# A hybrid attention and MLP layer on one core: how many steps of a side computation each attention unit carries

## The chip, the core and the metric

One core of a Trainium2 chip runs the whole layer in one launch. The core has a matrix engine (TensorE, PE in the profile, with its weight loads shown apart as PEld), a vector engine (VectorE, DVE), a scalar engine (ScalarE, ACT), a general engine (GpSimd, POOL) and an engine that here only issues transfers (SyncE, SP). Each engine works through its own queue in order. The metric is the device time of one execution in microseconds (us).

## What is computed

One trunk layer for a batch of one sequence: 2048 tokens of width 1024, all in float32. Cut to what matters here:

```
mod = silu(c) @ w_ada + b_ada                       # 1 x 6144, six parts of 1024
shift_a, scale_a, gate_a, shift_m, scale_m, gate_m = split(mod, 6)
h = rms_norm(x, g_attn) * (1 + scale_a) + shift_a
q_f, k_f, v_f, q_s, k_s, v_s, f_logit = split(h @ w_in)
o_fox = forgetting_attention(...)                   # 8 heads of 64, causal
o_sb  = stick_breaking_attention(...)               # 8 heads of 64, causal
x = x + gate_a * (concat(head_norm(o_fox), head_norm(o_sb)) @ w_out)
h = rms_norm(x, g_mlp) * (1 + scale_m) + shift_m
u_gate, u_val = split(causal_depthwise_conv(h @ w_up))
x = x + gate_m * ((silu(u_gate) * u_val) @ w_down)
return rms_norm(x, g_final)
```

The conditioning vector c is one row, so each of the six parts of mod is a product of a 1 x 1024 row with a 1024 x 1024 matrix. The first two parts (shift_a, scale_a) are needed at once and are computed at the start. The other four are the *late modulation*: gate_a (part 2 in the code), gate_m (part 5), shift_m (part 3) and scale_m (part 4). Gate_a is multiplied into the rows of w_out (with the head norms' gains), which then serves the output projection. The other three are needed only for the MLP.

## The kernel before

**Attention in 32 units.** A unit is one kind of attention ("sb" for stick-breaking, "fox" for forgetting), one pair of heads p (0 to 3) and one block tb of 512 queries (0 to 3). The list `units` (L807) has them in the order sb before fox, then p, then tb, so units 0 to 15 are sb and 16 to 31 are fox, and every fourth unit has the same tb. Attention is causal, so the work of a unit grows with tb: `tri` (L846) puts it at 10 + 16 tb, and `weight` (L843) puts an sb unit 1.4 times higher. `attend` (L697) is a generator that yields after each small stretch of a unit: logits, an elementwise stage on ACT, DVE and POOL, transposes on PE, copies out of PSUM, and products with the values.

**Projections beside it.** Each unit needs its queries and keys (and every second p also the values) projected from the normalized tokens. `proj` (L463) does it unit by unit: eight tiles `hp` of 512 KB are loaded from scratch memory `hs` (L468) and multiplied on PE (L342, L413). This runs ahead of attention: `pace` (L849) states how many projection steps should have been emitted at each point of a unit, and `follow` (L1058) emits them. For PE these products are the filler that runs while attention waits for ACT and DVE. The last projection ends in unit 26.

**The late modulation.** `late_mod` (L756) is a third generator. Its first step (the convolution's weights) is taken in unit 4 (L1035). After it come 55 steps:

- part 2: steps 1 to 8 each load one 128 x 1024 row block of w_ada (L776, 512 KB), scale it on ACT (L782, two halves) and add it into `wsum` on POOL (L783, two halves; the first block is L780 on POOL alone). Steps 9 and 10 sum over the partitions with two products on PE (L790) and add the bias (`gt`, loaded at L787) on DVE (L791)
- steps 11 to 26: `fold_out` (L743). Every second step loads a block of w_out (L746); every step scales half of it on DVE (L749), splits it into a high and a low float on ACT and POOL (L45, L46) and stores it to `wos` (L753)
- part 5: steps 27 to 34 are the loads and sums, 35 and 36 the products of the gate; then gt is stored to `gate_m` (L796)
- part 3: steps 37 to 44 are the sums, 45 the column sums on PE (L800, 16 small matmuls in the trace) with an addition on DVE
- part 4: steps 46 to 53 and 54 in the same way; step 55 is a last small operation on DVE

**One pool of ten tiles.** The projection's eight tiles and everything wide in the late modulation come from the same ten buffers named `hp`: `h_tile` (L155) and `wide` (L158), which is h_tile under another shape. A buffer is free again when the last instruction that reads it is done. So `wsum` holds one buffer from the first sum until the product on PE, and `gt` one from its load until it has been used up.

**Order of the instructions.** `interleave` (L109) decides in what order instructions are emitted. After each yield of attention it lets the projections follow and then takes steps from each filler: with k steps for a unit of n yields, step j (from 0) is taken after the first yield i for which (i + 1) k / n is above j. The framework then schedules each engine's queue with a simulation of its own, where the order of emission is the priority: an instruction that is ready and has its buffers can be put ahead of earlier ones that are not, on its own engine. The queues made this way are fixed when the program runs.

**After unit 29.** Ahead of unit 30 the rest of late_mod is drained (L1050), the pool of the hp tiles is closed, and the pool `big` takes its space; `first_mix` (L939) loads the folded w_out into it (`wo`, L948) during unit 30, and the output projection (L912) begins in unit 31.

```
for i, u in enumerate(units):
    ...
    interleave(attend(...), n, [(lm if i >= LATE else None, PER, False), (tail, ..., True)], follow)
```

with `LATE, PER = 12, 3` (L862): three steps in each of the units 12 to 29, which makes 54 by the end of unit 29, and the last one in the drain.

Of the kernel before, what the change touches and what calls it, by code (L numbers as in the profile page):

```python
# [34 lines left out]
def kernel(ctx: ExitStack, tc: tile.TileContext, x, c, w_ada, b_ada, g_attn, w_in, b_fgate,  # L35
# [69 lines left out]
    def drain(g):  # L105
        for _ in g:
            pass

    def interleave(main, n, fillers, follow):  # L109
        live = [[g, k, 0] for g, k, _ in fillers if g is not None]  # L110
        for i, _ in enumerate(main):
            tick()
            follow(i)
            for e in live:
                while e[2] < (i + 1) * e[1] / n:
                    e[2] += 1
                    if next(e[0], StopIteration) is StopIteration:
                        e[2] = 1 << 30
        for g, _, whole in fillers:
            if g is not None and whole:  # L120
                drain(g)
# [3 lines left out]
    def open_pool(name, side=None, space=None):  # L125
        st = pools[name] = ExitStack()
        kw = dict(space=space) if space is not None else {}
        return st.enter_context(tc.tile_pool(name=name, bufs=1, side=side, reuse_waits="tile", **kw))

    def close_pool(*names):  # L130
        for name in names:
            pools.pop(name).close()
# [84 lines left out]
    b = pv()  # L217
# [6 lines left out]
    for r, src in ((R_GA, g_attn), (R_GM, g_mlp), (R_GF, g_out_fox), (R_GS, g_out_sb), (R_BA, b_ada)):  # L224
        n = src.shape[1] // P
# [465 lines left out]
    def tick(n=1):  # L691
        for d in deferred:
            d[1] -= n
        while deferred and deferred[0][1] <= 0:
            deferred.pop(0)[0]()
# [111 lines left out]
    units = [(k, p, tb) for k in ("sb", "fox") for p in range(4) for tb in range(NTB)]  # L807
    weights = {}
    results = {}
# [16 lines left out]
    def attend_steps(u):  # L826
        kind, p, tb = u
        if kind == "fox":
            return sum(2 * (2 + 2 * tb + j2 + 1) for j2 in range(2)) + 1
        return sum(2 * (tb + 1 + 2 * tb + j2 + 1) for j2 in range(2)) + 1  # L830
# [3 lines left out]
    def project():  # L834
        for u in units[1:]:
            for _ in proj_gen(u):
                projected[0] += 1
                yield
            projected[1] += 1

    ahead = project()

    def weight(u):  # L843
        return 1.4 * tri(u[2]) if u[0] == "sb" else tri(u[2])

    def tri(tb):  # L846
        return 10 + 16 * tb
# [11 lines left out]
                      base + (total - base) * (done + weight(units[i]) * m / n) / span if i >= START else 0)  # L859

    LAG, ENDQ = 12, 16
    LATE, PER = 12, 3  # L862
    START, STOP = 3, 30

    HT = 2 * P
# [150 lines left out]
    IDLE = 6  # L1016
# [9 lines left out]
    lm = late_mod()  # L1026
    Fbs = None
    tail = None
    big = orp = None
    for i, u in enumerate(units):  # L1030
        kind, p, tb = u
        nxt = units[i + 1] if i + 1 < len(units) else None
        if u == ("sb", 1, 0):
            forget_sums()
            next(lm)  # L1035
        if u == ("fox", 0, 0):
            close_pool("sx")
            sx = open_pool("fx", side="right")
        if i == 14 or (kind == "fox" and tb == 0 and p):
            Fbs = load_sums(p if kind == "fox" else 0)  # L1040
        n = attend_steps(u)
        if i >= len(units) - 2:
            head_root(i - len(units) + 2)
            head_scale(i - len(units) + 2, pt(), sx)
        if nxt is None:
            tail = first_out()
        if i == len(units) - 2:
            for _ in ahead:
                projected[0] += 1
            drain(lm)  # L1050
            close_pool("sl", "psa")
            psc = open_pool("psc", side="right", space=PSUM)
            big = open_pool("big")
            orp = open_pool("orp")
            tail = first_mix()
        goals = list(pace(i))

        def follow(m):  # L1058
            while projected[0] < goals[min(m, n - 1)]:
                with tc.issue_after(marks[max(0, len(marks) - 1 - LAG)]) if START <= i < ENDQ else nullcontext():  # L1060
                    if next(ahead, 1) is not None:
                        break
            if nxt and projected[1] > i + 1 and loaded_units[0] == i + 1:
                loaded_units[0] += 1
                load_unit(*nxt, results[nxt[:2]])

        interleave(attend(kind, p, tb, results[kind, p], Fbs), n, [(lm if i >= LATE else None, PER, False), (tail, 17 + IDLE if nxt is None else 13, True)], follow)
        while nxt and loaded_units[0] == i + 1:
            next(ahead, None)
            follow(n)  # L1070
# [225 lines left out]
    for u in range(1, NU):  # L1296
        for c in range(8 if u == 1 else 0, 16):
            t, n, q = chunk(u, c)
# [8 lines left out]
    def bank_a():  # L1307
        return bank(psd, "o", 4)
# [138 lines left out]
    for sblk, order in enumerate(orders):  # L1447
# [21 lines left out]
        for n, ci in enumerate(order):  # L1469
# [5 lines left out]
            if not last_pair:  # L1475
                nxt = weights(n + 1)
            elif sblk == 0:
                load_h(1, 0)
                back = w_reload(SAVE[0])
                nxt = islice(back, 5)  # L1480
            else:
                nxt = None
# [12 lines left out]
        a, b = bank_a(), bank_a()  # L1495
# [189 lines left out]
    for i in range(7):  # L1685
        nxt = {}
        kept = []
        for s in range(2):
            banks = set_banks(s)
            xhs_ = [None] * 4  # L1690
            tail = []
            left = i in lefts
            if left:
                half, n = lefts[i]
                ops = left_over(s, half)
            for kp in range(NKP):
                a = ahead_a.pop((i, s, kp), None)
                if a is None:
                    a = a_operand(i, s, kp, raw_a())
# [63 lines left out]
```

## Time and profile before

| what | us |
|---|---|
| time, median of 3 runs | 2950.44 |
| lowest and highest of the runs | 2949.66, 2955.75 |
| span of the profiled execution, first to last instruction | 2941.4 |
| the median run's time less the profiled span | 9.0 |
| PE busy in the span | 2867.8 |
| ends of units 11, 14, 15, 17, 18, 19 (store of the unit's output, L740) | 686.0, 801.5, 882.8, 922.7, 978.5, 1058.9 |
| ends of units 23 to 26 | 1217.1, 1241.8, 1283.6, 1337.3 |
| ends of units 27 to 31 | 1379.4, 1391.0, 1419.1, 1453.7, 1516.9 |
| first and last load of w_ada by late_mod (L776) | 629.7, 1308.4 |

The profile is of one execution, and its engines' rows say how much of the span each was at work. PE is busy almost throughout; what matters are the few places where it isn't. The span is what the views below divide up; the time of a run has some 9 us more around it. After attention (from 1516.9 us) come the output projection and the MLP, where the change does nothing.

### The profile page before, as it was taken

The page shows a single profiled execution, that of the slowest core. Times are in us where ns is not written, and L with a number is a line of the kernel's source. Part 1 is how long each engine was busy: PE and PEld are TensorE (multiplying, and loading weights), DVE is VectorE, ACT ScalarE, POOL GpSimd, SP SyncE. Part 2 cuts the span into 40 slices and gives each one's busy share as a digit, 9 for nine tenths or more (in the row PEclk, how much of TensorE's full clock was granted, in tenths as well). Part 3 has the DMA queues.
Part 4 walks back from the last instruction along what each step waited for, and adds up shares of the span by engine and source line. Part 5 has one row for each costly group of instructions (what it writes and reads, how often), then busy time and mean ns, then how long its engine had stood idle before and what let it go on. Part 6 is the DMA issues. An engine that isn't in the chain of part 4 may idle for free.

```text
span 2941.4 us, 45922 instructions
## 1 busy us (share of the span) xinstructions
PE 2867.8 (97%) x15772; PEld 2459.7 (84%) x15772; DVE 2179.5 (74%) x3464; ACT 1686.0 (57%) x3187; POOL 901.1 (31%) x967
## 2 busy tenths in 40 slices
PE   8999999999999999999999999999999999999998
PEld 7888888888988988888888788888788888888887
DVE  5787778877886656658843788888998888575476
ACT  5776767677776656658744554444444445433342
POOL 0431322243032423231213344444254543142200
PEclk8999999999999999999999999999999999999999
DMA  9749756867469794794537775554754444975644
GB/s 293 255 139 321 236 188 207 301 211 229 162 212 356 269 277 139 232 323 140 182 120 233 245 232 128 130 136 129 236 132 125 130 130 132 309 257 185 216 158 151
DMA packets 348346, 601.89 MB, mean 205 GB/s; under 512 B 34672, under 2 KB 178800, under 8 KB 348112
## 3 DMA queue, kind: packets, MB, share of 16 engines
q1 hardware_dynamic: 324208, 558.06, 57.7%
q0 software_dynamic: 10880, 20.97, 4.3%
q10 hardware_dynamic: 13024, 19.93, 1.9%
q8 instruction: 124, 2.03, 0.3%
q14 instruction: 110, 0.90, 0.1%
HBM read 420.77 MB, written 177.02 MB: 203 GB/s over the span
## 4 chain that ended last, share of the span: by engine, by line
PE 46%; DMA 3%; DVE 2%; SPq 1%; ACT 1%; issue 1%; POOL 0%; DVEq 0%; ACTq 0%; POOLq 0%
PE ps_o L1315 19%; PE ps_t L1315 7%; PE ps_o L1614 6%; PE ps_t L1614 3%; PE ps_bc L1614 3%; PE ps_o L912 1%; PE ps_pv L615 1%; DMA r<-rstd 1%; PE ps_bc L912 1%; PE ps_pt L606 1%; PE ps_o L1609 1%; DMA wo<-wos 1%; DMA hm<-hf_m 1%; SPq L895 1%; DVE op L46 1%
## 5 line engine op out<-in xcount | busy, mean ns | idle before, releaser
L1315 PE MATMUL ps_o<-op,wu 128*128 128x512 f32 x2592 | 608.0, 389 | 2.0 <-DVE snap L1366 1.5
L1315 PEld LDWEIGHTS ps_o<-op,wu 128*128 128x128 f32 x2592 | 486.2, 188 | 103.9 <-DVE snap L1366 1.9
L611 DVE TENSOR_TENSOR at<-ps_pt,at 128x512 fp32r<-128x512 f32 (+1 forms) x576 | 366.1, 652 | 100.2 <-ACT at L610 97.3
L636 DVE TENSOR_TENSOR_SCAN a<-r,a 128x512 f32<-128x512 f32 (+2 forms) x320 | 368.3, 1167 | 77.8 <-ACT a L631 39.9
L342 PE MATMUL ps_pj<-hp,w_qk 128*128 128x512 f32 x1512 | 411.2, 403 | 14.5 <-DMA hp<-hs 12.9
L610 ACT ACTIVATE at<-ps_pt 128x512 fp32r<-128x512 f32 (+1 forms) x576 | 318.5, 576 | 139.1 <-PE ps_pt L606 123.1
L615 PE MATMUL ps_pv<-at,V 128*128 128x256 f32 x2216 | 386.8, 292 | 9.3 <-DVE at L611 4.2
L615 PEld LDWEIGHTS ps_pv<-at,V 128*128 128x128 f32 x2216 | 320.9, 190 | 39.8 <-DVE at L611 11.4
L342 PEld LDWEIGHTS ps_pj<-hp,w_qk 128*128 128x128 f32 x1512 | 275.4, 190 | 71.0 <-DMA hp<-hs 16.2
L45 ACT ACTIVATE wu<-wuraw 128x512 fp32r<-128x512 f32 x204 | 128.9, 632 | 248.5 <-PE ps_o L1315 190.1
L596 PE MATMUL ps_qk<-K,Q 128*128 128x512 f32 (+2 forms) x640 | 265.7, 416 | 5.6 <-ACT a L631 3.3
L413 PE MATMUL ps_pj<-w_v,hp 128*128 128x256 f32 (+1 forms) x1536 | 236.6, 288 | 2.1 <-DVE hp L422 1.6
L597 PE MATMUL ps_qk<-K,Q 128*128 128x512 f32 (+2 forms) x640 | 235.7, 369 | 0.0
L1315 PE MATMUL ps_t<-op,wu 128*128 128x512 f32 x888 | 220.8, 390 | 1.0 <-DVE op L46 1.0
L413 PEld LDWEIGHTS ps_pj<-w_v,hp 128*128 128x128 f32 x1536 | 209.0, 189 | 10.9 <-DVE q L373 1.5
L630 ACT ACTIVATE r<-ps_qk 128x512 f32<-128x512 f32 (+2 forms) x320 | 173.1, 541 | 58.2 <-PE ps_qk L597 55.5
L46 DVE TENSOR_TENSOR wu<-wuraw,wu 128x512 fp32r<-128x512 f32 x204 | 189.6, 930 | 18.1 <-ACT wu L45 16.7
L1315 PEld LDWEIGHTS ps_t<-op,wu 128*128 128x128 f32 x888 | 166.4, 188 | 36.5 <-DVE op L46 1.8
L606 PE MATMUL ps_pt<-edge,a 128*128 128x128 f32 x1088 | 185.1, 274 | 8.4 <-DVE a L636 7.8
L1614 PE MATMUL ps_o<-op 128*128 128x512 f32 x840 | 191.5, 389 | 0.0
L1614 PEld LDWEIGHTS ps_o<-op 128*128 128x128 f32 x840 | 157.7, 188 | 32.7
L679 ACT ACTIVATE p<-p,mn 128x128 f32<-128x128 f32 (+15 forms) x128 | 153.9, 1203 | 53.3 <-DVE mn L675 52.2
(342 smaller groups left out, 5237.6 us busy)
## 6 DMA issues: line engine op xcount, KB each, us to landing
hp<-hs SPq DMA_DIRECT2D x224, 512.0 KB
wuraw<-in_w_up_dram SPq DMA_DIRECT2D x80, 512.0 KB
ra<-g SPq DMA_DIRECT2D x136, 256.0 KB
rb<-in_w_down_dram SPq DMA_DIRECT2D x108, 256.0 KB
g<-u SPq DMA_DIRECT2D x80, 256.0 KB
hs<-hp SPq DMA_DIRECT2D x32, 512.0 KB
hp<-in_w_ada_dram SPq DMA_DIRECT2D x32, 512.0 KB
qk_fox<-q SPq DMA_DIRECT2D x32, 512.0 KB
```

The lines of the kernel that those rows point to most:

```text
L46: (lo_engine or nc.gpsimd).tensor_sub(lo, src, f(hi))
L342: nc.tensor.matmul(acc, w[kt][:, a, n], h[:, bb], start=kt == 0 and i == 0, stop=kt == KT - 1 and i == 2)
L413: nc.tensor.matmul(av[:, t * width:(t + 1) * width], hts[kt][:, a, tok], w[1][kt][:, bb, 0:width], start=kt == 0 and m == 0, stop=kt == KT ...
L596: nc.tensor.matmul(b[:, :cw], Q[:, hl, 0, qcols], K[:, hl, :cw], start=True, stop=False)
L597: marks.append(nc.tensor.matmul(b[:, :cw], Q[:, hl, 1, qcols], K[:, hl, :cw], start=False, stop=True).ins)
L606: nc.tensor.transpose(b[:, i * P:(i + 1) * P], blk(kts[kk], qi), ident)
L610: copies = [nc.scalar.activation(at[:, 0, lo:], b[:, lo:], AF.Copy).ins, nc.vector.tensor_sub(at[:, 1, lo:], b[:, lo:], f(at[:, 0, lo:])).ins]
L611: nc.vector.tensor_sub(at[:, 1, lo:], b[:, lo:], f(at[:, 0, lo:])).ins]
L615: m = nc.tensor.matmul(o[:, 0:2 * P], V[kt // 4][:, kt % 4, hl, :], rhs, start=first and kk == 0 and w == 0, stop=last and kk == 1 and w == 1)
L636: nc.vector.tensor_tensor_scan(rev, r[:, 0:need][:, ::-1], rev, 0.0 if right[qi] is None else right[qi][:, 0:1], ALU.mult, ALU.add)
L1315: nc.tensor.matmul(b, w[:, p, j], o[:, q], start=first and i == 0, stop=last and i == 2, skip_group_check=True)
L1614: nc.tensor.matmul(b, a[:, p, t * P:(t + 1) * P], w[:, q], start=first and i == 0, stop=last and i == 2, skip_group_check=True)
```

## The change

The constant three is replaced by a number of steps for each unit, `late_steps(i)`, and the steps are spread over units 12 to 28 in proportion to `weight`:

```diff
+    def late_steps(i):
+        upto = [sum(weight(u) for u in units[LATE:max(LATE, min(v, LATE_END))]) for v in (i, i + 1, LATE_END)]
+        a, b = (round(LATE_STEPS * v / upto[2]) for v in upto[:2])
+        return b - a
+
...
-    LATE, PER = 12, 3
+    LATE, LATE_END, LATE_STEPS = 12, 29, 55
...
-        interleave(attend(kind, p, tb, results[kind, p], Fbs), n, [(lm if i >= LATE else None, PER, False), (tail, 17 + IDLE if nxt is None else 13, True)], follow)
+        interleave(attend(kind, p, tb, results[kind, p], Fbs), n, [(lm, late_steps(i), False), (tail, 17 + IDLE if nxt is None else 13, True)], follow)
```

The weights of units 12 to 28 sum to 608.4, and the cumulated, rounded share of 55 gives these numbers (in the column "emitted", the steps taken by the end of the unit, before and after):

| unit | kind, p, tb | steps before | steps after | emitted before | emitted after |
|---|---|---|---|---|---|
| 12 | sb 3 0 | 3 | 1 | 3 | 1 |
| 13 | sb 3 1 | 3 | 4 | 6 | 5 |
| 14 | sb 3 2 | 3 | 5 | 9 | 10 |
| 15 | sb 3 3 | 3 | 7 | 12 | 17 |
| 16 | fox 0 0 | 3 | 1 | 15 | 18 |
| 17 | fox 0 1 | 3 | 2 | 18 | 20 |
| 18 | fox 0 2 | 3 | 4 | 21 | 24 |
| 19 | fox 0 3 | 3 | 6 | 24 | 30 |
| 20 | fox 1 0 | 3 | 0 | 27 | 30 |
| 21 | fox 1 1 | 3 | 3 | 30 | 33 |
| 22 | fox 1 2 | 3 | 4 | 33 | 37 |
| 23 | fox 1 3 | 3 | 5 | 36 | 42 |
| 24 | fox 2 0 | 3 | 1 | 39 | 43 |
| 25 | fox 2 1 | 3 | 2 | 42 | 45 |
| 26 | fox 2 2 | 3 | 4 | 45 | 49 |
| 27 | fox 2 3 | 3 | 5 | 48 | 54 |
| 28 | fox 3 0 | 3 | 1 | 51 | 55 |
| 29 | fox 3 1 | 3 | 0 | 54 | 55 |

No instruction is added or removed; the steps are emitted at other places.

## The prediction

> **What bounds the kernel now.** I read the page first, then who made PE wait in the stretch where the late modulation runs, then those waits in order of time, then a table of stretches, and last SP's queue.
>
> ```profile
> span 2941.4 us, 45922 instructions
> ...
> PE 2867.8 (97%) x15772; PEld 2459.7 (84%) x15772; DVE 2179.5 (74%) x3464; ACT 1686.0 (57%) x3187; POOL 901.1 (31%) x967
> ...
> PEclk8999999999999999999999999999999999999999
> ```
>
> PE is at work 97% of the span at nearly full clock, and the change adds and removes no instruction. So it can only win or lose time in which PE stands still or runs slowly. The waits of PE from 600 to 1420 us (units 11 to 29; columns: total us, times, longest):
>
> ```profile
> PE ps_pj L342 <- DMA hp<-hs: 12.3, 7, 6.0
> ```
>
> It is the largest row: a projection waits for its tiles, the tiles that share ten buffers with the late modulation. The three long ones of the fox units, from PE's timeline:
>
> ```profile
> 1052.80 0.80 PE L342 MATMUL ps_pj<-hp,w_qk 128*128 128x512 f32 x1 [6.01 <-DMA hp<-hs]
> ...
> 1155.19 1.66 PE L342 MATMUL ps_pj<-hp,w_qk 128*128 128x512 f32 x6 [0.47 <-DMA hp<-hs]
> 1208.81 0.79 PE L342 MATMUL ps_pj<-hp,w_qk 128*128 128x512 f32 x1 [3.40 <-DMA hp<-hs]
> ```
>
> A stall costs more than its length, as the table of stretches shows (length, then busy us of PE, PEld, DVE, ACT, POOL, then granted clock, DMA share, GB/s):
>
> ```profile
> 1040.00:1052.80 12.80, 6.79 (x54) 6.26 (x52) 5.45 (x16) 6.55 (x17) 2.20 (x4) 0.93 1.03 307
> 1052.80:1058.90 6.10, 6.10 (x20) 5.15 (x21) 1.04 (x4) 1.31 (x3) 0.30 (x1) 0.58 1.05 275
> ...
> 1208.80:1217.00 8.20, 8.19 (x37) 7.49 (x38) 3.61 (x9) 5.73 (x16) 3.52 (x4) 0.63 0.65 250
> ...
> 1167.70:1195.00 27.30, 27.09 (x192) 24.22 (x191) 26.14 (x66) 20.93 (x35) 3.77 (x7) 1.00 0.25 81
> ```
>
> After the stall in unit 19 the clock is 0.58 for 6.1 us: 6.1 x 0.42 = 2.6 us lost on top of 6.0. After the one in unit 23 it is 0.63 for 8.2 us: 8.2 x 0.37 = 3.0 us on top of 3.4. The two have different causes: DMA is full (a share of 1.03) ahead of the first, and nearly idle (0.25) ahead of the second.
>
> **Why unit 23 stalls.** SP's loads of one projection's tiles (L468) between 1120 and 1201 us, grouped, with the times of the first and the last; then pieces of SP's queue: the ends of units 21 and 22 (L740), the bias's load (L787), the seventh tile, the gate's store (L796) and the eighth tile:
>
> ```profile
> L468 SPq DMA_DIRECT2D hp<-hs x8: 319/339/450, 1126.7 to 1200.7; - x8
> ```
>
> ```profile
> 1087.76 0.73 SPq L787 DMA_DIRECT2D hp<-in_b_ada_dram  x1
> ...
> 1115.10 0.32 SPq L740 DMA_DIRECT2D os<-oT  x1
> ...
> 1151.16 0.34 SPq L468 DMA_DIRECT2D hp<-hs  x1
> ...
> 1167.74 0.34 SPq L740 DMA_DIRECT2D os<-oT  x1
> ...
> 1198.70 0.33 SPq L796 DMA_DIRECT2D gate_m<-hp  x1
> ...
> 1200.74 0.33 SPq L468 DMA_DIRECT2D hp<-hs  x1
> ```
>
> POOL's first sums of parts 5 and 3, and the products on PE that end part 5's gate and part 4's column sums:
>
> ```profile
> 1003.89 1.57 POOL L780 TENSOR_SCALAR hp<-hp,cs 128x512 f32<-128x512 f32 x1 [2.81 <-DMA hp<-in_w_ada_dram]
> ...
> 1129.54 3.12 POOL L780 TENSOR_SCALAR hp<-hp,cs 128x512 f32<-128x512 f32 x2 [2.66 <-PE ps_qk L597]
> ```
>
> ```profile
> 1179.91 1.02 PE L790 MATMUL ps_pt<-hp,ones 128*128 128x512 f32 x2
> ...
> 1195.49 1.02 PE L790 MATMUL ps_pt<-hp,ones 128*128 128x512 f32 x2
> ...
> 1403.53 1.84 PE L800 MATMUL ps_pt<-ones,hp 128*128 128x1 f32 x16
> ```
>
> Count the buffers at 1151: seven tiles of the projection are loaded; part 5's wsum has one since 1003.9, its gt since 1087.8, part 3's wsum since 1129.5. That is ten. The eighth tile, wanted after the six products of 1155.2, is loaded at 1200.7, once the gate's products (1179.9, 1195.5) have let wsum go. In between the projection stands still; L342's instructions on PE alone, in the table of stretches (length, PE busy, clock, DMA share, GB/s):
>
> ```profile
> 1155.70:1208.80 53.10, 1.15 (x5) 0.99 0.46 130
> ```
>
> That is 1.15 us of projection in 53. So the sums run early, as soon as buffers allow, while the products that free the buffers run where they are emitted. I check that: steps 35 and 36 are taken in unit 23 (1167.7 to 1217.1) after 33% and 67%, which is 1184 and 1200; they ran at 1180 and 1195. Step 54 in unit 29 (1391.0 to 1419.1) after 67% is 1410; it ran at 1404. The place of emission tells when PE's steps run, within some 6 us.
>
> **The change, part by part.**
>
> *Part 5's gate.* Its loads and POOL's additions, grouped (duration ns min/median/max, first and last start):
>
> ```profile
> L776 SPq DMA_DIRECT2D hp<-in_w_ada_dram x8: 328/333/628, 997.9 to 1077.2; - x8
> ...
> L783 POOL TENSOR_TENSOR hp<-hp x14: 1290/1298/1308, 1011.5 to 1082.8; 128x512 f32<-128x512 f32 x14
> ```
>
> Steps 35 and 36 move to unit 22 (1115.1 to 1167.7), after 25% and 50% of it: 1128 and 1141. The two buffers come free some 55 us earlier, before the eighth tile is due. The stall goes: 3.4 idle + 3.0 of slow clock + 0.5 at 1155.2 = 6.9 us. Is PE then late for something else? PE takes its queue in a fixed order, so products that met an unfinished sum would hold attention's matmuls behind them and with them ACT and DVE; the sums must be ready by 1128. They were done by 1082.8 + 1.3 = 1084, and are emitted earlier now. What is late next is attention's own chain; what filler in the empty 53 us would save further I leave at 0, since PE shows busy 27.09 of 27.30 us in 1167.7 to 1195 without any. **-6.9**, from 0 (another tile is late there) to -6.9.
>
> *Part 5's sums and unit 19.* Ahead of 1052.8 the load of the last three tiles stands in SP's queue behind transfers that take long on full DMA engines:
>
> ```profile
> 1041.12 4.49 SPq L363 DMA_DIRECT2D K<-qk_fox  x4
> 1045.92 2.54 SPq L468 DMA_DIRECT2D hp<-hs  x3
> ```
>
> ```profile
> L753 SPq DMA_DIRECT2D wos<-hp x16: 525/560/871, 802.9 to 997.3; - x16
> ```
>
> Part 5's eight loads of 512 KB (4.2 MB, 14 us at the 307 GB/s above) run beside them from 998 to 1077, right behind fold_out's last store at 997.3. After the change fold_out's last step is in unit 19 after 17% instead of unit 20 after 33%, and steps 27 to 30 are in unit 19. So the burst can begin some 10 to 20 us sooner, if fold_out ends sooner. It then collides less at 1040, but it stays in unit 19, and SP's order is new. I take half of the stall's 6.0 + 2.6: **-4**, from -8.6 to +8.6 (a second one like it).
>
> *Fold_out in unit 15.* Seven steps are emitted there instead of three. DVE and ACT are loaded there (units 15, then 16 with 17; below, fold_out's operations on DVE in unit 15):
>
> ```profile
> 801.50:882.80 81.30, 76.37 (x515) 67.93 (x514) 67.45 (x109) 63.88 (x140) 24.89 (x34) 1.00 0.67 222
> 882.80:922.70 39.90, 39.82 (x254) 35.09 (x253) 30.27 (x79) 26.93 (x54) 11.48 (x16) 1.00 1.04 370
> ```
>
> ```profile
> L749 DVE SCALAR_TENSOR_TENSOR hp<-hp,cols 128x512 f32<-128x512 f32 x4 | 2.8, 748 | 1.7 <-DMA hp<-in_w_out_dram 1.7
> ```
>
> Four steps of fold_out already ran in unit 15, pulled forward, so three more come: 3 x 0.75 = 2.2 us on DVE, 3 x 0.43 waiting for w_out (1.7 over 4). Projections cover part of it. **+1.5**, from 0 to +3.5. The steps that leave units 16 and 17 win nothing: PE is busy 39.82 of 39.90 us there.
>
> *Part 4's column sum.* It moves from unit 29 (1403.5) to unit 27 (1337.3 to 1379.4) after 80%, 1371. The chain of waits goes through it:
>
> ```profile
> 1403.69 1.68 PE ps_pt L800 x16
> ...
> 1406.40 6.35 DMA wo<-wos
> ```
>
> ```profile
> 1379.40:1419.10 39.70, 37.35 (x260) 31.74 (x259) 33.77 (x99) 32.65 (x65) 8.60 (x18) 1.00 0.69 220
> 1419.10:1453.70 34.60, 31.96 (x216) 26.98 (x214) 31.34 (x84) 28.74 (x54) 10.15 (x16) 1.00 0.60 196
> ```
>
> The loads of wo can begin 30 us earlier and clear SP before first_mix. But wo is used in unit 31, after 1453.7, and PE's idle time from unit 28 to 30 is 2.35 + 2.64 us in all, with DVE busy 85 to 91%. **-1**, from 0 to -5.0. Part 3's column sum moves from unit 26 to unit 25 and frees a buffer; no tile is late there now: 0. Part 2's gate products stay in units 14 and 15 or move into the end of 14: 0, from -2.4 (what is left of the 12.3 us) to +2.4.
>
> Sum: -6.9 - 4 + 1.5 - 1 = -10.4 us on the profiled span of 2941.4, which becomes 2931; with the 9.0 us around it, 2940 against the median of 2950.4.
>
> *A rule against the rows.* The Trainium skill (TensorE: Matmul & The Clock Gate, Part 1) says that PE falls to half clock after an idle window of about 3.4 us and is back at full clock after about 3.4 us of work. By that a stall would cost half of 3.4, 1.7 us as an estimate, beyond its length, the first term 5.6 instead of 6.9, the second 3.9, and the sum -9.0. The rows show 2.6 and 3.0, so I keep those.
>
> **The rivals.**
>
> *The stall only moves* (to 2949): the change does not do what it says, since the sums float anyway. Ten buffers for eight tiles and up to three wide ones stay ten; with steps emitted in units 19 and 23 in greater number, another eighth tile can be late in place of this one. For it: the 12.3 us are seven waits, not one. Against: the holders are let go earlier everywhere. Then only -1 is left.
>
> *Slower by DMA* (to 2959). DMA is full in units 16 and 17 (1.04 in the row above) and nearly so in 18:
>
> ```profile
> 922.70:978.50 55.80, 55.80 (x335) 49.16 (x334) 35.48 (x84) 30.32 (x57) 12.83 (x17) 1.00 0.93 337
> ```
>
> If fold_out ends early enough for part 5's 4.2 MB to go out ahead of the tiles that SP loads up to 975, that is 12 us of transfers at 337 GB/s ahead of a projection without spare buffers: a stall like that of 1052.8, 8.6 us, with nothing won elsewhere. It decides from a first load of part 5 before about 970; before the change it was 998. With unit 23's gain beside it, 2952.
>
> *Slower by POOL and DVE* (2952 to 2959). POOL's sums take longer beside stick-breaking (620 to 750 us, first row) than beside fox (1120 to 1330):
>
> ```profile
> L783 POOL TENSOR_TENSOR hp<-hp 128x512 f32<-128x512 f32 x14 | 21.3, 1541 | 20.7 <-ACT hp L782 20.7
> ...
> L783 POOL TENSOR_TENSOR hp<-hp 128x512 f32<-128x512 f32 x28 | 35.7, 1294 | 22.6 <-ACT hp L782 19.7 <-issue 2.8
> ```
>
> ```profile
> L783 POOL TENSOR_TENSOR hp<-hp x56: 1267/1293/2204, 644.6 to 1322.3; 128x512 f32<-128x512 f32 x56
> ```
>
> If it is DVE that holds POOL up and the reverse, three more steps in unit 15 could hold DVE by up to 3 x (0.75 + 2.2) = 8.8 us (2.2 for the longest sum, 2204 ns). DVE has 81.3 - 67.5 = 13.8 us to spare, so it decides only if the holds fall into the scan's chain. The Trainium skill (SBUF — State Buffer, Who interferes with whom) says that a DVE instruction with two SBUF inputs contends with a GpSimd instruction that reads SBUF; by that rule, the two means above agree in direction, and no run here shows the lock itself.
>
> **How the numbers follow.** Forecast 0.48; the stall moves 0.27; DMA 0.17; POOL and DVE 0.08. A measurement of this kernel can tell about 0.2%, 5.9 us, from no change: 2944.5 to 2956.3. The forecast's own range, 2931 to 2947, is mostly below it (0.42 of 0.48); the second rival lies mostly inside (0.24 of 0.27); of the last two 0.16 of 0.25 is above. That makes 0.46 faster, 0.36 the same, 0.18 slower. The range from 2930 to 2960 takes in all bounds but both stalls gone with every other term at its best, and two new stalls.
>
> **What would show it.** Right: L790's second pair near 1130 to 1145, all eight tiles of that projection loaded by 1150, no wait of L342 above 2 us in unit 23, clock 1.00 there, L800's last group near 1370. Wrong: L342's waits again above 10 us in total, elsewhere; or a clock under 0.9 in units 16 to 19; or unit 15 longer than 84 us.

## The result and the profile after

| what | before | after |
|---|---|---|
| median of 8 runs, us | 2949.55 | 2958.06 |
| lowest and highest | 2939.44, 2955.75 | 2955.62, 2965.59 |
| ratio, 95% interval | | 1.0032 [1.0021, 1.0042] |
| a second set of runs, ratio (median 2954.91) | | 1.0024 [1.0015, 1.0034] |

The change makes the kernel slower by 7 to 9 us; the forecast was 10.4 us faster. All runs count here and below but one, a slow one of g2 (3810.77 us at a granted clock of 0.69). The page of the changed kernel, whose profiled run took 2959.57 us:

```profile
span 2957.1 us, 45920 instructions
...
PE 2871.1 (97%) x15772; PEld 2467.8 (83%) x15772; DVE 2182.6 (74%) x3464; ACT 1682.5 (57%) x3187; POOL 911.0 (31%) x967
...
PEclk9999999999999999999999999999999999999999
```

The work is the same, as the counts show. PE is busy 3.3 us longer than before and stands idle 12.4 us longer (span less busy: 73.6 before, 86.0 after).

**Where the time came from.** A unit's store moves against its work, so the stretches here are cut at the same point of the program in every kernel: where DVE has written the last output of units 10, 15, 19, 26 and 30. First the kernel before, then the changed one, in the table of stretches (length, then busy us of PE, PEld, DVE, ACT, POOL, then granted clock, DMA share, GB/s):

```profile
607.60:873.50 265.90, 253.16 (x1695) 225.42 (x1693) 207.53 (x280) 198.57 (x432) 79.78 (x97) 1.00 0.61 197
873.50:1058.40 184.90, 178.26 (x1124) 158.44 (x1124) 119.09 (x299) 113.86 (x226) 59.64 (x79) 0.98 0.91 308
1058.40:1336.90 278.50, 273.64 (x1818) 246.88 (x1817) 179.30 (x462) 177.54 (x339) 86.32 (x112) 0.99 0.70 231
1336.90:1453.20 116.30, 110.78 (x772) 96.04 (x771) 102.22 (x278) 95.49 (x183) 26.29 (x49) 1.00 0.61 192
sum 845.60, PE 815.85 PEld 726.78 DVE 608.15 ACT 585.45 POOL 252.04; mean PE 203.96 PEld 181.69 DVE 152.04 ACT 146.36 POOL 63.01
```

```profile
612.30:883.70 271.40, 256.30 (x1690) 229.22 (x1688) 214.67 (x288) 200.25 (x439) 89.12 (x101) 0.97 0.62 202
883.70:1065.80 182.10, 175.45 (x1111) 156.74 (x1111) 113.38 (x286) 113.08 (x221) 61.37 (x79) 0.98 0.89 302
1065.80:1347.10 281.30, 276.47 (x1832) 249.24 (x1831) 179.92 (x468) 175.12 (x337) 79.62 (x108) 0.99 0.69 226
1347.10:1470.30 123.20, 112.39 (x776) 99.79 (x774) 102.14 (x278) 96.11 (x183) 26.16 (x49) 0.96 0.59 181
sum 858.00, PE 820.61 PEld 735.00 DVE 610.11 ACT 584.56 POOL 256.28; mean PE 205.15 PEld 183.75 DVE 152.53 ACT 146.14 POOL 64.07
```

From unit 11 to unit 30 the changed kernel takes 12.4 us longer: +5.5 in units 11 to 15, -2.8 in 16 to 19, +2.8 in 20 to 26, +6.9 in 27 to 30. PE's busy time alone grows by 4.8 for (nearly) the same instructions: the clock in units 11 to 15 is 0.97 in place of 1.00, so 256.3 us of work hold what 253.2 held. In the second execution of the changed kernel the four stretches are 271.2, 181.3, 280.6 and 117.6, so the last +6.9 are not in every execution. The other 3.3 us between the two spans lie where the change moves no step: +4.7 ahead of unit 11, -1.4 behind unit 30.

**How much two traces can differ by chance.** Up to 664 us every engine's queue is the same in all twenty traces of this case, and the stretch ahead of unit 11 takes 607.6 to 621.8 us. Five of them (the kernel before, e2, e4, e6, e8 below) have the same queues on through unit 15, but for one small instruction on POOL, and take 263.1 to 269.1 us for units 11 to 15. A difference of some 6 us in one stretch of two traces can be scatter. Five traces with the changed kernel's queues in units 11 to 15 take 268.8 to 271.4 us.

**The gate's products went where the forecast put them, and the stall came back elsewhere.** The changed kernel's products of part 5, and its loads of tiles from 1120 us (duration ns min/median/max, first and last start):

```profile
L790 PE MATMUL ps_pt<-hp,ones x4: 590/592/592, 1126.2 to 1136.3; 128*128 128x512 f32 x4
```

```profile
L468 SPq DMA_DIRECT2D hp<-hs x17: 319/376/1196, 1137.0 to 1237.1; - x17
```

The products are 50 us earlier and the eighth tile is loaded at 1137 in place of 1200.7: the count of buffers was right. But PE's waits from 600 to 1440 us (total, times, longest) read

```profile
PE ps_pj L342 <- DMA hp<-hs: 13.2, 5, 5.6
PE ps_pv L615 <- DVE oT L738: 8.2, 2, 7.4
PE ps_pt L606 <- DVE a L636: 6.9, 10, 1.9
```

against 12.3 of L342 before. Unit 19 still holds one of 5.6, and the one of unit 23 is now in PE's timeline 18 us later, and costs the clock what it did before (0.60 for 8.5 us, with DMA now full):

```profile
1226.75 1.04 PE L342 MATMUL ps_pj<-hp,w_qk 128*128 128x512 f32 x3 [3.02 <-DMA hp<-hs]
1229.09 1.65 PE L342 MATMUL ps_pj<-hp,w_qk 128*128 128x512 f32 x3 [1.30 <-DMA hp<-hs]
```

```profile
1220.00:1227.50 7.50, 4.47 (x36) 3.98 (x34) 2.73 (x11) 5.31 (x11) 2.50 (x5) 1.00 1.01 308
1227.50:1236.00 8.50, 7.20 (x31) 6.15 (x31) 2.91 (x5) 2.28 (x6) 1.11 (x1) 0.60 1.04 293
```

The other two rows are new or larger: 7.4 us of waiting for oT in unit 29, and twice as much waiting for the scan (a, L636), which in the kernel before reads

```profile
PE ps_pt L606 <- DVE a L636: 3.6, 7, 1.1
```

The experiments take up both.

### The profile page after: what moved, and what is told of

The parts are those of the page before. It is cut to its first block, busy times and chain, and to the rows that moved or that the text cites. A ratio compares the mean times of both kernels' runs of the same rounds, so it can differ in the third digit from the quotient of the medians.

```text
span 2957.1 us, 45920 instructions
## 1 busy us (share of the span) xinstructions
PE 2871.1 (97%) x15772; PEld 2467.8 (83%) x15772; DVE 2182.6 (74%) x3464; ACT 1682.5 (57%) x3187; POOL 911.0 (31%) x967
## 4 chain that ended last, share of the span: by engine, by line
PE 48%; DMA 2%; DVE 2%; ACT 1%; issue 1%; SPq 0%; POOL 0%; DVEq 0%; ACTq 0%; POOLq 0%
PE ps_o L1320 20%; PE ps_t L1320 8%; PE ps_o L1619 6%; PE ps_t L1619 3%; PE ps_bc L1619 3%; PE ps_o L917 2%; PE ps_pv L615 1%; PE ps_pt L606 1%; PE ps_bc L917 1%; DMA r<-rstd 1%; PE ps_o L1614 1%; PE ps_qk L596 1%; PE ps_qk L597 1%; DMA os<-oT 0%; DMA x1s<-x1u 0%
## 5 line engine op out<-in xcount | busy, mean ns | idle before, releaser
L342 PE MATMUL ps_pj<-hp,w_qk 128*128 128x512 f32 x1512 | 417.1, 405 | 17.6 <-DMA hp<-hs 13.8
L636 DVE TENSOR_TENSOR_SCAN a<-r,a 128x512 f32<-128x512 f32 (+2 forms) x320 | 370.3, 1173 | 82.1 <-ACT a L631 42.0
L342 PEld LDWEIGHTS ps_pj<-hp,w_qk 128*128 128x128 f32 x1512 | 274.9, 191 | 72.7 <-DMA hp<-hs 16.3
```

The costliest lines, as they stand in the source:

```text
L342: nc.tensor.matmul(acc, w[kt][:, a, n], h[:, bb], start=kt == 0 and i == 0, stop=kt == KT - 1 and i == 2)
L636: nc.vector.tensor_tensor_scan(rev, r[:, 0:need][:, ::-1], rev, 0.0 if right[qi] is None else right[qi][:, 0:1], ALU.mult, ALU.add)
```

## The experiments

Three theories at first. A: wo's loads, set free earlier, stand ahead of unit 27's store in SP's queue, and attention waits for the buffer of oT. B: the moved sums cost projection waits in units 12 to 26. C: the loss is spread, a part of it in units 12 to 15. Where an edit changes only numbers of steps, they are given in words as a map from unit to steps; a unit that is not named keeps its own.

**The last units (theory A).** SP's queue of the changed kernel, then the wait that follows on DVE and on PE, and the clock:

```profile
1389.16 1.89 SPq L953 DMA_DIRECT2D wo<-wos  x3
...
1392.03 1.76 SPq L953 DMA_DIRECT2D wo<-wos  x2
...
1394.57 8.76 SPq L953 DMA_DIRECT2D wo<-wos  x7
1403.97 1.28 SPq L740 DMA_DIRECT2D os<-oT  x1
```

```profile
1417.80 0.42 DVE L738 TENSOR_TENSOR oT<-ps_pv,o 64x256 f32<-64x256 f32 x1 [6.64 <-DMA os<-oT]
```

```profile
1409.00:1418.28 9.28, 1.85 (x14) 1.35 (x13) 2.13 (x7) 3.97 (x6) 0.29 (x1) 0.84 1.06 298
1418.28:1425.00 6.72, 6.72 (x39) 6.39 (x40) 4.75 (x12) 4.32 (x9) 1.01 (x2) 0.72 0.93 276
```

Unit 27's store is issued at 1403.97, behind twelve loads of wo (3 + 2 + 7), and with DMA full (1.06) it lands so late that oT, with two buffers, can't be written until 1417.80. Four kernels test what that is worth: the changed kernel again; the column sum of part 4 put back to unit 29; the same sum pulled forward in the kernel before; and the loads ordered behind a store.

```diff
+        return {27: 4, 28: 0, 29: 2}.get(i, b - a)             # e1, in the changed kernel
```

```diff
+ (lm if i >= LATE else None, {27: 9, 28: 1, 29: 0}.get(i, PER), False)   # e2, in the kernel before
```

```diff
+        stores.append(nc.sync.dma_start(os_[mp][tb], oT).ins)  # e3, in the changed kernel
...
+                    with tc.issue_after(stores[28]):
+                        nc.sync.dma_start(f(wo[p][i // 4]), ...)
```

> The changed kernel once more, unedited, so that the other runs stand beside it on one chip. Theory A (loads of wo ahead of the store, a stall at the end of unit 28): the trace again has a wait of PE on oT of 5 to 9 us near 1410 to 1420, and the time is 1.003 of before. If that wait was chance of the one profiled execution: no wait above 2 us there, and the time is 1.003 all the same.

> The changed kernel, but steps 54 and 55 (part 4's column sum on PE and the small operation after it) are kept back to unit 29, where they stood before; all other steps as changed. Theory A (the loss comes from the loads of wo, which the early column sum sets free in unit 27 and which stand ahead of unit 27's store in SP's queue): no wait of DVE above 2 us on the store of oT, the 7.4 us wait of PE in unit 29 and the half clock behind it are gone, 2948 to 2951, ratio to before 0.999 to 1.001. Theory B (the loss comes from projections that wait for their tiles in units 12 to 26): still 2957 to 2959.

> The kernel before with three steps in each unit up to 26, and the last ten steps taken early: nine in unit 27, one in unit 28, none in unit 29. Theory A: loads of wo ahead of unit 27's store, a wait of 5 to 8 us on oT in unit 29, 2957 to 2959, ratio 1.002 to 1.003. Theory B: as before, 2949 to 2951.

> The changed kernel with the loads of wo queued behind the store of unit 28's output on SP, everything else as changed. Theory A: no wait on oT, 2948 to 2951, ratio 0.999 to 1.001. Theory B: 2957 to 2959.

Measured: 1.0024 [1.0015, 1.0034]; e1 1.0022 [1.0010, 1.0033]; e2 1.0010 [0.9997, 1.0023]; e3 1.0041 [1.0027, 1.0055]. In PE's waits from 1340 us the wait for oT is gone in e3:

```profile
PE ps_pv L615 <- DVE oT L739: 1.3, 1, 1.3
```

and e3 is no faster for it. The second execution of the changed kernel has 2.1 us of it. So A is a true stall of some executions, not what makes the median slower. A third buffer for oT wasn't tried.

**One part alone (theory B, C).** The gate of part 5 early, the early part (units 12 to 17), the middle part (units 18 to 26), and the kernel before without most of the sums:

```diff
+ {21: 5, 22: 4, 23: 0}.get(i, PER)                              # e4, in the kernel before
+ {12: 1, 13: 4, 14: 5, 15: 7, 16: 1, 17: 0}.get(i, PER)         # e5, in the kernel before
+ return {12: 3, 13: 3, 14: 3, 15: 3, 16: 3, 17: 4, 18: 5, 27: 4, 28: 0, 29: 2}.get(i, b - a)   # e6, in the changed kernel
+                if kt and part != 2:                            # e8, in the kernel before
+                    yield
+                    continue
```

> The kernel before with part 5's gate alone moved from unit 23 to unit 22: five steps in unit 21, four in unit 22, none in unit 23, three in all others. The prediction's first term: the 3.4 us wait in unit 23 and its half clock go, 2942 to 2945, ratio 0.998. Rival (the wait only moves to the next projection): the gate's products run near 1141 and 1154, but L342 still waits 10 us or more in total from 600 to 1420 us, 2948 to 2952.

> The kernel before with the change's steps in units 12 to 15 alone (1, 4, 5, 7), then 1, 0 and three each, so that from unit 18 on it is the kernel before. Theory C (the loss is spread, and a third of it comes from the steps pulled into the stick-breaking units 12 to 15): 2950 to 2953, ratio 1.001, and the stretch from unit 11 to 15 takes 269 to 272 us in the trace against 266 to 269. Theory A or B: as before, 2948 to 2950, ratio 0.999 to 1.001.

> The changed kernel with three steps in each of the units 12 to 16, then 4 and 5, the change's own steps in units 19 to 26, four in unit 27 and the last two in unit 29: the middle of the change alone. Theory B (projections wait in units 16 to 26): 2953 to 2957, ratio 1.002, L342's waits 12 us or more. Theory A or C: 2948 to 2951, ratio 0.999 to 1.001.

> The kernel before without 21 of the 24 loads and sums of parts 5, 3 and 4 (only the first row block of each is loaded and summed, so gate_m, shift_m and scale_m are partial); all steps stay where they are, and wsum and gt hold their buffers as long as before. If the waits of L342 come from the loads and the buffers of single blocks: they fall from 12 us to under 4, and the time to 2936 to 2942. If they come from wsum and gt holding buffers until their products on PE: the wait in unit 23 stays (3 us or more there), the one in unit 19 goes, 2941 to 2946.

Measured: e4 1.0012 [1.0001, 1.0023], e5 1.0030 [1.0019, 1.0041], e6 1.0045 [1.0032, 1.0057], e8 0.9994 [0.9979, 1.0008]. In e4 the gate's products run at 1136 to 1151, and PE's waits from 600 to 1440 us read

```profile
PE ps_pj L342 <- DMA hp<-hs: 12.7, 8, 4.1
```

So the gate's place alone wins nothing: the wait is had by another tile. e8, which leaves out 21 of the 24 loads and sums of parts 5, 3 and 4, brings this row down to 5.4 us, and the time doesn't follow beyond its interval: these waits, the center of the forecast, seem worth little. (The traced execution was e8's fastest, 2936.64 us beside a median of 2948.00, so the row may not hold for the others.) The early part alone is as slow as the whole change, which leaves theory C. But the middle part alone is no less slow, with the early steps where they were: its trace is 8.8 us longer than before from unit 11 to 30 (854.4), all of it behind unit 15 (189.1 us in units 16 to 19, 280.9 in 20 to 26, 118.9 in 27 to 30). The parts do not add up (e5 and e6 together would be +7.5 per mille).

**The early part taken in two.** It holds part 2's sums and gate in units 12 to 14, and five steps of fold_out more emitted in unit 15. Theory S: the fold_out steps among the stick-breaking units are the loss. All in the kernel before, but f3:

```diff
+ {12: 1, 13: 4, 14: 5, 15: 2}.get(i, PER)                       # f1: sums early, fold_out kept back
+ {15: 8, 16: 1, 17: 0}.get(i, PER)                              # f2: fold_out early, sums kept
+ {14: 2, 15: 0, 16: 5, 17: 5}.get(i, PER)                       # f4: fold_out later than before
```

```diff
+            raw, ready = ready, block(kt + 1) if kt < KT - 1 else None   # f3, in the changed kernel's fold_out
```

> Edit: before, with 1, 4, 5, 2 steps in units 12 to 15 and three in every other unit, so the sums and the gate of part 2 are emitted as in the early part of the change, but unit 15 ends after 12 steps as before and no fold_out step is emitted earlier than before. Theory S (the loss of the early part is fold_out among the stick-breaking units: VectorE stands in its queue for w_out's load and the scan behind it is late): within 0.1% of before (2947 to 2951), and PE's waits for DVE's a in units 11 to 15 as in before (about 3 us on the transposes), against 1.0030 for the whole early part. Rival (any other order of emission costs something, by chance clock windows): again slower by 0.2 to 0.4% (2954 to 2960).

> Edit: before, with 8, 1, 0 steps in units 15, 16, 17 and three in every other unit, so only fold_out's steps 13 to 17 are emitted in unit 15 instead of units 16 and 17. Theory S: slower by 0.2 to 0.35% (2954 to 2959), units 12 to 15 some 3 us longer than in before, with DVE waiting longer for w_out's tiles. Rival (the sums of units 13 and 14 cause it, or the order by chance): within 0.1% of before (2947 to 2951).

> Edit: the changed kernel, with fold_out's load of each w_out block emitted one block ahead of its use, so that the steps stay where the change puts them. Theory S with DVE's wait for the load as its mechanism: DVE's waits for w_out in units 14 and 15 go from 4.4 us to under 1.5 us and the time falls by 2 to 4 us against the changed kernel (2953 to 2956). Rival (DVE's added work and the splits on POOL hold the scan, not the load): no gain, 2957 to 2960; the extra buffer that is held may also make a projection wait and cost 3 to 8 us more.

> Edit: before, with 2, 0, 5, 5 steps in units 14, 15, 16, 17 and three in every other unit, the opposite of the change: all of fold_out is emitted behind the stick-breaking units. Theory S: units 12 to 15 are some 1 to 3 us shorter than in before, and 0 to 3 us of it come back as projection waits in units 16 to 18, where DMA is full: 2945 to 2950. Rival (every order but the old one is slower): 2952 to 2960.

Measured: **f1 0.9966 [0.9957, 0.9976]**, 2939.74 us, faster than both kernels; f2 1.0012 [0.9997, 1.0027]; f4 1.0010 [0.9995, 1.0025]; f3 1.0042 [1.0026, 1.0058]. f1 and e5 differ only in where five steps of fold_out are emitted, and lie 6.4 per mille apart, on two chips. Early sums are a gain; early sums with early folds are a loss; early folds alone cost nothing clear of noise. (A step that is emitted earlier need not run earlier, as its queue and its buffers allow: of the 16 fold_out steps, DVE has run 8 by the end of unit 15 in e5 and in f2, and 6 in the kernel before and in f1.) f3 leaves DVE's wait for w_out in units 14 and 15 where it was (5.7 us in f3, 4.6 in the changed kernel). In f1 it is 2.1, but in its second trace (g2, below) 4.2 beside 4.4 in e5's second (g4), so that wait is not what sets the two apart.

Then f1 and e5 again side by side on one chip, half of the folds in between, and the changed kernel without the early folds:

```diff
+ {12: 1, 13: 4, 14: 5, 15: 4, 16: 2, 17: 2}.get(i, PER)         # g3, in the kernel before
+        return {15: 2, 16: 3, 17: 3}.get(i, b - a)              # g1, in the changed kernel
```

> Edit: none against f1 (1, 4, 5, 2 steps in units 12 to 15, then three). If its gain was real: 0.995 to 0.998 (2936 to 2945). If it was chance: 0.999 to 1.002.

> Edit: f1 with 4, 2, 2 steps in units 15, 16, 17 in place of 2, 3, 3: two fold_out steps more in unit 15, where the whole early part has five more. Theory S: between the two, 0.998 to 1.002 (2942 to 2955), PE's waits for DVE's a in unit 15 between 0.9 and 4.4 us. Rival (each order of emission gives its own time, whatever its steps): outside of that, or the waits as in f1 and the time not.

> Edit: none against the early part alone (1, 4, 5, 7, 1, 0 steps in units 12 to 17, then three). Theory S: 1.002 to 1.004, and slower than g2 on the same chip by 10 to 20 us, all of it in units 11 to 19. Rival (chance): within 5 us of g2.

> Edit: the changed kernel with 2, 3, 3 steps in units 15, 16, 17 in place of 7, 1, 2, so that after unit 17 it has emitted as many as the change (18 against 20 before unit 18, 2 fewer to the end) and fold_out stays where it was. Theory S (fold_out pulled into the stick-breaking units is the loss): faster than the changed kernel by 10 us or more, 2940 to 2949. Rival (the later part of the change costs as much by itself, as the kernel with the middle part alone, at 1.0045, says): 2953 to 2960.

| steps in units 15, 16, 17 (after 1, 4, 5) | us | ratio |
|---|---|---|
| 2, 3, 3 (g2) | 2941.50 | 0.9980 [0.9969, 0.9990] |
| 4, 2, 2 (g3) | 2947.71 | 0.9999 [0.9988, 1.0010] |
| 7, 1, 0 (g4) | 2953.74 | 1.0014 [1.0005, 1.0023] |
| 2, 3, 3, then as the change (g1) | 2944.02 | 0.9982 [0.9972, 0.9991] |

Each fold_out step that is emitted earlier costs: by medians 6.2 us for the first two, 6.0 for the next three, 12.2 in all; by means 10.9 us in all, give or take 2.9. The first row also says that f1's gain is real, if nearer to 0.2% than to 0.34%. The change without the early folds is faster than the kernel before by 4.5 us and than the change by some 11 to 14 us. (g1 differs from it in one more thing: it is two steps later from unit 18 on, so part 4's column sum comes at 1414 us, behind unit 29. By e1 the column sum is worth a fraction of this; the two steps in between were not tried by themselves.)

Where the time is, in g4 and then in g2, whose traced executions lie 17.9 us apart (2956.18 and 2938.31):

```profile
614.40:883.20 268.80, 254.84 (x1690) 227.37 (x1688) 215.34 (x289) 200.54 (x440) 89.71 (x101) 0.98 0.62 206
883.20:1078.20 195.00, 191.59 (x1224) 171.72 (x1225) 116.65 (x292) 115.63 (x228) 62.60 (x81) 0.99 0.88 299
...
sum 850.50, PE 819.95 PEld 731.75 DVE 611.13 ACT 584.51 POOL 256.82; mean PE 204.99 PEld 182.94 DVE 152.78 ACT 146.13 POOL 64.20
```

```profile
611.40:874.80 263.40, 251.19 (x1698) 226.05 (x1696) 210.52 (x284) 198.42 (x435) 83.15 (x98) 1.00 0.62 201
874.80:1058.80 184.00, 180.93 (x1153) 161.21 (x1154) 118.14 (x298) 115.52 (x227) 61.84 (x80) 1.00 0.91 311
...
sum 836.60, PE 809.30 PEld 724.44 DVE 607.34 ACT 584.93 POOL 254.84; mean PE 202.32 PEld 181.11 DVE 151.84 ACT 146.23 POOL 63.71
```

The sums differ by 13.9 us, and 10.7 of them are PE *busy* (819.95 less 809.30). PE does the same products but for one, more slowly, for the most part since the clock falls to half after waits (0.98 and 0.99 in these rows of g4, 1.00 in those of g2); only 3.2 us are idle time. In the other pair, e5 and f1, the sums differ by 8.9 us (847.9 and 839.0), 6.1 of them busy. (The second stretch is 11 us longer in g4 partly because more of the projection is done in it, 1224 matmuls against 1153.) A view of waits alone would show a quarter to a third of this.

**How a fold_out step makes PE wait.** At the end of unit 15 the changed kernel runs two scans while POOL runs the subtractions of two fold_out steps. From the timelines of POOL, DVE and PE, and the table of stretches:

```profile
870.13 3.79 POOL L46 TENSOR_TENSOR hp<-hp 128x512 fp32r<-128x512 f32 x2 [2.34 <-ACT hp L45]
```

```profile
870.57 4.44 DVE L636 TENSOR_TENSOR_SCAN a<-r,a 128x512 f32<-128x512 f32 x2
```

```profile
873.02 0.66 PE L606 MATMUL ps_pt<-edge,a 128*128 128x128 f32 x2 [1.92 <-DVE a L636]
...
875.07 0.69 PE L606 MATMUL ps_pt<-edge,a 128*128 128x128 f32 x2 [1.18 <-DVE a L636]
```

```profile
872.50:879.30 6.80, 4.88 (x20) 4.22 (x21) 6.17 (x12) 2.13 (x5) 2.12 (x3) 0.50 1.04 334
```

Two scans of this size take 2 x 1.29 = 2.6 us by the mean in the kernel before; here they take 4.44. PE waits 1.92 and 1.18 us for them. Its clock is at half for 6.8 us, of which it works 4.88: 2.4 us lost on top of 3.1. (In the 3.4 us ahead of that, 869.1 to 872.5, PE was at work for only 1.16.) In units 14 and 15 together, the scans on DVE and the subtractions on POOL, first before, then after:

```profile
L636 DVE TENSOR_TENSOR_SCAN a<-r,a 128x512 f32<-128x512 f32 x42 | 53.6, 1289 | 12.0 <-ACT a L631 8.4 <-POOL a L633 3.3
...
L46 POOL TENSOR_TENSOR hp<-hp 128x512 fp32r<-128x512 f32 x6 | 9.4, 1574 | 22.1 <-ACT hp L45 22.1
```

```profile
L636 DVE TENSOR_TENSOR_SCAN a<-r,a 128x512 f32<-128x512 f32 x42 | 57.9, 1391 | 10.5 <-ACT a L631 8.1 <-POOL a L633 2.3
...
L46 POOL TENSOR_TENSOR hp<-hp 128x512 fp32r<-128x512 f32 x8 | 14.5, 1825 | 17.2 <-ACT hp L45 17.1
```

Both grow: the scan by 102 ns in the mean, the subtraction by 251. All scans of the changed kernel's units 14 and 15 (min/median/max):

```profile
L636 DVE TENSOR_TENSOR_SCAN a<-r,a x52: 408/1283/2301, 747.4 to 872.8; 128x512 f32<-128x512 f32 x42, 128x384 f32<-128x384 f32 x4, 128x128 f32<-128x128 f32 x3, 128x256 f32<-128x256 f32 x3
```

The longest is 2.30 us beside a median of 1.28. Before, the longest was 1.58, but g2, with the sums alone early, has one of 2.26 too; in the kernel before and in g2:

```profile
L636 DVE TENSOR_TENSOR_SCAN a<-r,a x52: 408/1281/1584, 744.5 to 864.6; 128x512 f32<-128x512 f32 x42, 128x384 f32<-128x384 f32 x4, 128x128 f32<-128x128 f32 x3, 128x256 f32<-128x256 f32 x3
```

```profile
L636 DVE TENSOR_TENSOR_SCAN a<-r,a x52: 407/1274/2264, 744.3 to 865.9; 128x512 f32<-128x512 f32 x42, 128x384 f32<-128x384 f32 x4, 128x128 f32<-128x128 f32 x3, 128x256 f32<-128x256 f32 x3
```

So such holds stand in the fastest kernel as well; the early folds make them more. PE waits 5.3 us for the scan in g4's units 14 and 15, 3.5 in g2's and 1.2 in f1's. The Trainium skill (SBUF — State Buffer, Who interferes with whom) says that a DVE instruction with two SBUF inputs and a GpSimd instruction that reads SBUF contend; these rows show it for this pair.

Theory L: that hold is what the early folds cost. The test is to take POOL's part out of fold_out, in the changed kernel (h1) and in g1 (h2):

```diff
-                split(w[:, 0], w[:, 1], raw[:, n * TB:(n + 1) * TB])
+                for half in range(2):
+                    nc.scalar.activation(w[:, half], raw[:, n * TB:(n + 1) * TB], AF.Copy)
```

> Edit: the changed kernel, in which fold_out writes its low half with a second copy on ACT in place of the subtraction on POOL; the low float of the folded w_out is left out by that. Theory L: no scan in units 14 and 15 above 1.35 us, PE's waits for DVE's a there under 3 us in place of 5.1, and the time within 5 us of h2 (the changed kernel is 14 us above g1): about 2940 to 2948. Rival: the scans become shorter, but the time stays 8 us or more above that of h2: 2950 to 2958.

> Edit: g1 (the change with 2, 3, 3 steps in units 15, 16, 17) with the same copy on ACT in place of POOL's subtraction in fold_out, whose low float is left out. Theory L: 0 to 5 us faster than g1 (2939 to 2944), since fewer of its scans had the subtraction beside them; h1 within 5 us of it. Rival: as g1, 2944, and h1 8 us or more above it.

Measured: h1 1.0052 [1.0037, 1.0067], 2966.25 us; h2 0.9985 [0.9974, 0.9996], 2944.33 us. The same view of h1's scans, and the stretches of h1 and then of h2 (units 11 to 15, 16 to 19, 20 to 26):

```profile
L636 DVE TENSOR_TENSOR_SCAN a<-r,a x52: 415/1275/1306, 745.8 to 867.9; 128x512 f32<-128x512 f32 x42, 128x384 f32<-128x384 f32 x4, 128x128 f32<-128x128 f32 x3, 128x256 f32<-128x256 f32 x3
```

```profile
613.00:877.70 264.70, 253.12 (x1690) 227.78 (x1690) 209.11 (x284) 203.19 (x444) 74.13 (x92) 0.99 0.63 209
877.70:1058.30 180.60, 174.53 (x1107) 153.66 (x1106) 115.65 (x293) 118.78 (x234) 52.13 (x74) 1.00 0.87 296
1058.30:1344.60 286.30, 279.67 (x1838) 251.18 (x1836) 177.12 (x463) 175.41 (x336) 78.55 (x107) 0.99 0.67 227
```

```profile
608.30:871.20 262.90, 252.65 (x1700) 227.70 (x1699) 208.50 (x285) 201.53 (x442) 71.33 (x93) 0.99 0.62 202
871.20:1059.30 188.10, 177.85 (x1110) 157.72 (x1109) 117.33 (x292) 118.29 (x232) 47.77 (x70) 0.97 0.88 301
1059.30:1334.00 274.70, 271.88 (x1825) 246.64 (x1824) 179.09 (x463) 177.07 (x340) 83.56 (x111) 1.00 0.69 232
```

Without POOL's subtraction no scan is longer than 1.31 us, and units 11 to 15 take 264.7 us in place of 271.4. Kernels with sums and folds early take 268.8 to 271.4 us there, those with the sums alone early (f1, g1, g2) 263.4 to 266.2, and h1 lies in the second group. So the hold is real, and what the early folds cost in this stretch, some 6 us between the two groups, seems to go with the subtraction; one trace of h1 doesn't settle how much of it. But theory L said that h1 would come within 5 us of h2 in time, and it is 22 us above it, further than the changed kernel is above g1. From unit 16 to 26 it is 4.1 us longer (466.9 against 462.8), and in units 27 to 30 the wait for oT is back (PE's waits):

```profile
PE ps_pv L615 <- DVE oT L738: 8.1, 1, 8.1
```

That makes 11 of the 22.8 us between the two spans; 4.7 lie ahead of unit 11, where the queues are the same, and 6.8 behind unit 30. So the hold of the scan is not the price of early folds in the time of a run, and theory L falls as an account of it. What follows the folds in the queues (when buffers come free, when part 5's loads and later wo's go out) differs from kernel to kernel, and I can't show which part of it is theirs.

**What stays open.** How much of the 12 us is the scan and how much is the order that follows. Why early sums are a gain. Why the middle part alone (e6) costs 4.5 per mille with the folds kept back, while g1, with a middle part that is two steps later behind earlier sums, is 1.8 per mille faster than before. Why h1 is slower than the changed kernel, by 11 us.

## Why the prediction was wrong

**The sign was wrong because of the term "Fold_out in unit 15", +1.5 from 0 to 3.5.** It counted three more steps there by DVE's own 0.75 us each and the wait for w_out. The trace has two more (8 in units 14 and 15, 6 before), and emitting five of them earlier costs some 12 us in time (g4 against g2); without that the change is a gain (g1, 0.9982). So the place of the folds, put at 1.5 us, is the term that turned the sign, and the two gains it was to be set against did not come (below). What the term had no place for is that POOL's subtraction lengthens the scan, that the transposes on PE wait for the scan with nothing to fill in, and that such waits of 1 to 2 us cost nearly as much again in clock (2.4 on 3.1). The traces show that for units 11 to 15, where kernels with and without early folds lie some 6 us apart. As the mechanism of the whole it isn't shown: without the subtraction early folds cost 22 us (h1 against h2). Nor do the folds account for every loss, since the middle part alone loses without them (e6). The last rival, "slower by POOL and DVE" (2952 to 2959), named that mechanism, put up to 8.8 us on it and said what it hung on, whether the holds fall into the scan's chain; it was given 0.08. What spoke for it stood in the prediction: sums of 1541 ns beside stick-breaking and 1294 beside fox. It was read for the sums of POOL, whose early place is a gain in f1, and not for the scan on the other side of the same hold.

**"Part 5's gate", -6.9.** The products moved to 1126 and the eighth tile to 1137, as stated. The step that failed is the answer to "is PE then late for something else?": another tile was, at 1226.75 (3.0 + 1.3 us and 0.60 of clock for 8.5 us). The rival "the stall only moves" was right for this term, and e4 shows it by itself: no gain. I took the lower end, 0, for the less likely one on the ground that PE was busy in 27.09 of 27.30 us; that says that filler isn't missed there, not that the tile behind it comes in time.

**"Part 5's sums and unit 19", -4.** The stall is 5.6 us where it was 6.0. Part 5's first load went out at 974.0 in place of 997.9, just short of the "before about 970" of the DMA rival, and the clock in units 16 to 19 is 0.98 as before: no second stall came of it either.

**"Part 4's column sum", -1.** It ran at 1379, not 1371, and "clear SP before first_mix" was wrong in sign: the loads went ahead of a store that attention needs. 0 to 7 us, by execution; e1 and e3 bound its part of the median as small.

**The 9.0 us around the span** were not around it: the changed kernel's profiled run took 2959.57 us with a span of 2957.1, 2.5 us. So the profiled execution of before must have been quicker than its median run, and the difference was to be read as scatter between executions.

**The price of a stall in clock.** 2.6 and 3.0 us per stall were kept, and the runs bear that out: 2.9 us in the 8.5 us behind 1226.75 (7.20 us at work x 0.40), and 2.4 us behind waits of only 1.9 and 1.2 us. By the Trainium skill (TensorE: Matmul & The Clock Gate, Part 1) it would have been 1.7, as an estimate, and behind an idle window of about 3.4 us; the trace has half clock for 6.8 us, behind 3.4 us in which PE was at work for 1.16 and no single wait was above 1.92. The forecast counted clock only for the two large stalls, and none for the small waits which fold_out added.

## What to carry to other kernels

A share by weight assumes that a step costs the same wherever it is put. Before side work is moved, ask of each of its instructions, on every engine, which chain it will stand beside: here the sums could go early with a gain, and the fold steps behind them could not. A mechanism that a trace shows, here the POOL part that slows a DVE scan, need not be what the time hangs on: leaving it out did not bring the time back. Where an even change does nothing or harm, take its parts one at a time: the early sums alone (1, 4, 5, 2 steps, then three) beat both kernels, at 0.9966 and 0.9980. And a count of waits on PE understates a loss where the clock answers to waits: compare PE's busy time for the same instructions. Before a difference of a few microseconds between two traces is explained, look at a stretch in which they do the same.

## What the runs showed of the hardware

Waits shorter than 2 us went with 6.8 us at a clock of 0.50 (from 872.5 us), which cost 2.4 us on top of 3.1 us of waits. The same queues took 607.6 to 621.8 us ahead of unit 11. A scan on DVE and a subtraction on POOL held each other up to 2.30 us and 2.21 us; without the subtraction no scan took over 1.31. The 2.21 is POOL's longest among the eight of the changed kernel's units 14 and 15.
